# An mLSTM mixer's causal table added chunk by chunk, one maximum with a scalar operand, one scaling on ScalarE

## The chip, the core and the metric

One core of a Trainium2 chip runs the whole program. The metric is the device time of one execution, in microseconds (us). The core has five engines that run side by side, each in the order of its own queue: TensorE (PE, with its weight loads as PEld), VectorE (DVE), ScalarE (ACT), GpSimd (POOL) and SyncE (SP), which here issues the DMAs.

## What is computed

Two decoder layers, each a pre-normed mixer with two head groups in parallel: sliding-window attention and four mLSTM heads, both gated and joined by one output projection. The change lies in the mLSTM, which is computed in chunks of time:

```
D = where(causal, b[t] - b[s] + log_i[s], NEG)            # exponents of a chunk
m_t = maximum(a_t, D.max(-1))
S = (q k^T) * exp(D - m_t)
num = exp(a_t - m_t) * (q C_in) + S v
den = exp(a_t - m_t) * (q n_in) + S.sum(-1)
h = num / maximum(abs(den), exp(-m_t))
h = rms_norm(h, out_norm_g)                               # over the 256 values of a head
C, n, m = state after the chunk                           # scan over the chunks
```

There are 1040 rows of time (16 meta tokens and 1024 tokens), 4 heads with keys of 128 and values of 256.

## The kernel before

All matmuls that need fp32 accuracy are split: each operand is a high part and a low part, both rounded to a faster 32-bit format, and three matmuls take the place of one. ACT makes the high part by a copy, POOL or DVE the low part by a subtraction. Weights come in by DMA (`raw`), ACT copies the high part into `RING` (L159), and POOL subtracts (L160). A projection (L183) is a chain of 24 matmuls into one of two PSUM banks `pj`; an engine must read the bank out before the next but one projection can begin. These readers are L793 (values), L819 (inputs of the convolution) and L838, L841 and L842 (gates).

Time is cut into nine chunks: chunk 0 has the 16 meta rows, chunks 1 to 8 have 128 rows each. A layer runs the attention first, interleaved with its projections, and then, head by head, the mLSTM. `weave` puts the small tasks of one head's mLSTM (`m_tasks`) between the projections that the next head needs (`v_tasks`, `conv_tasks`) and those of the gates (`mo_tasks`). The tasks of a head are `begin`, and then `sa(c)`, `sb(c - 1)` and `sc_(c - 2)` for each chunk.

`begin` (L857) allocates `EB`, 128 partitions by 9 chunks by 128 columns. One DMA fills it with the negated running maxima of the head, the same on every partition, from a scratch tensor `em` in DRAM. Then one addition on POOL (L861) adds the causal table `tri` (0 where s <= t, -1e30 elsewhere) to all nine chunks at once.

`sa(c)` splits the values (ACT L877, POOL L878), turns and scales the keys (L881, L883, L884), updates the state (L887, then L891), splits the queries (L896, L897), takes the exponential of the chunk's part of `EB` (ACT L899), multiplies it with the scores (L901, L902) and splits the product (L905, L906).

`sb(c)` splits the state for the next chunk (ACT L911, POOL L912), multiplies the scores with the values and the queries with the state (both L867), and joins the two in `num` (ACT L925, DVE L929): 256 columns of values and in column 256 the sum `den`. A chain on one column follows, in a tile `s4` of four columns: the larger of `-den` and the bound (DVE L932), the larger of that and `den` (DVE L933), the reciprocal (L934), the sum of squares of the row (ACT L935), two steps of arithmetic (L936, L937), a power of -1/2 on POOL (L938), a product (L939), and last the scaling of the 256 columns of `num` by the result (DVE L941). `sc_(c)` turns the scaled rows on TensorE (L951), and ACT writes them out with the norm's weight (L954).

DVE also computes the convolution (L821, L824, L827), of which ACT's tanh (L826) is a part, and POOL multiplies with the gates (L606).

What sets the order: in the attention stage TensorE's instructions keep the order of the program (`pin`). In the mLSTM stage they do not: there a planner at compile time sets the order on every engine, by priority in the order of the program and by its own estimate of when each instruction can start. On the chip each engine then keeps to that order: an instruction that has to wait holds all that stands behind it in its queue.

Of the kernel before, what the change touches and what calls it, by code (L numbers as in the profile page):

```python
# [14 lines left out]
AF = mybir.ActivationFunctionType  # L15
ALU = mybir.AluOpType
# [46 lines left out]
def build(ctx, tc, I, O):  # L63
    nc = tc.nc
    ve, sc, gp, pe, sy = nc.vector, nc.scalar, nc.gpsimd, nc.tensor, nc.sync
    in_order = [False]

    def pin(ins):

        return tc.keep_in_program_order(ins) if in_order[0] else ins  # L70
# [25 lines left out]
    def bank(tag):  # L96
        return bp[tag].tile([128, 512], F32, name=tag)
# [22 lines left out]
    def unit(dt=F32):  # L120
        return up.tile([128, UW], dt, name="u")
# [4 lines left out]
    def p512(dt, n=512):  # L126
        return ptp.tile([128, 516], dt, name="p512")[:, :n]

    def w1k(dt=F32):
        return wkp.tile([128, 272], dt, name="w1k")  # L130
# [11 lines left out]
    tri = cp.tile([128, 128], F32, name="tri")  # L142
# [210 lines left out]
    for l in range(DEPTH):  # L353
# [500 lines left out]
        def m_tasks(h, st):  # L854
            live = {}

            def begin():  # L857
                EB = unit()[:, :].rearrange("p (c t) -> p c t", c=9)
                st["EB"] = EB
                sy.dma_start(EB, em[l].rearrange("(c h) t -> h c t", h=4)[h].partition_broadcast(128))  # L860
                gp.tensor_tensor(EB, EB, tri.rearrange("p (a t) -> p a t", a=1).to_broadcast([128, 9, 128]),  # L861
                                 op=ALU.add)
                st["Y"] = [unit() for _ in range(2)]

            def mm_split(out, a, b):
                for i, (x, y) in enumerate(((a[0], b[0]), (a[0], b[1]), (a[1], b[0]))):
                    pin(pe.matmul(out, x, y, start=(i == 0), stop=(i == 2)))  # L867

            def sa(c):
                t0, p = TT[c]  # L870
                r = 4 * c + h
                C0, C1 = Cb[c % 3], Cb[(c + 1) % 3]
                v = st["V"](c)[:p, :]
                qc, kc = st["q"][:, t0:t0 + p], st["k"][:, t0:t0 + p]
                KQ, VV = p512(F32R), p512(F32R, 516)
                V = VV[:p, 0:258], VV[:p, 258:516]
                sc.activation(V[0], v, AF.Copy)  # L877
                gp.tensor_tensor(V[1], v, V[0], op=ALU.subtract)  # L878
                if c < 8:
                    pk = bank("pt")  # L880
                    pin(pe.transpose(pk[:p, 0:128], kc, ident))  # L881
                    kt = KQ[:p, 0:128], KQ[:p, 128:256]
                    sc.activation(kt[0], pk[:p, 0:128], AF.Copy, scale=TK[:p, 2, r:r + 1])  # L883
                    ve.scalar_tensor_tensor(kt[1], pk[:p, 0:128], TK[:p, 2, r:r + 1], kt[0],  # L884
                                            ALU.mult, ALU.subtract)
                    pu = bank("pss")
                    mm_split(pu[:, 0:258], kt, V)  # L887
                    if c == 0:
                        ve.tensor_copy(C1, pu[:, 0:258])
                    else:  # L890
                        ve.scalar_tensor_tensor(C1, C0, AC[:, r:r + 1], pu[:, 0:258], ALU.mult, ALU.add)  # L891
                if c < first_q:
                    return
                q = KQ[:, 256:256 + p], KQ[:, 384:384 + p]
                if c > 0:
                    sc.activation(q[0], qc, AF.Copy)  # L896
                    gp.tensor_tensor(q[1], qc, q[0], op=ALU.subtract)  # L897
                De = w1k()
                sc.activation(De[:p, :p], st["EB"][:p, c, :p], AF.Exp, bias=TK[:p, 3, r:r + 1])  # L899
                pS = bank("pss")  # L900
                pin(pe.matmul(pS[:p, :p], kc, qc, start=True, stop=True))  # L901
                ve.tensor_tensor(De[:p, :p], pS[:p, :p], De[:p, :p], op=ALU.mult)  # L902
                DR = w1k(F32R)
                dr_ = DR[:p, 0:p], DR[:p, 128:128 + p]
                sc.activation(dr_[0], De[:p, :p], AF.Copy)  # L905
                ve.tensor_tensor(dr_[1], De[:p, :p], dr_[0], op=ALU.subtract)  # L906
                live[c] = q, V, dr_

            def split_state(c):
                ch, cl = Cr[c % 2]  # L910
                sc.activation(ch, Cb[c % 3], AF.Copy)  # L911
                gp.tensor_tensor(cl, Cb[c % 3], ch, op=ALU.subtract)  # L912

            def sb(c):
                if c + 1 < 9:
                    split_state(c + 1)
                if c < first_q:
                    return
                t0, p = TT[c]
                r = 4 * c + h  # L920
                q, V, dr_ = live.pop(c)
                num = w1k()
                pn = bank("po")
                mm_split(pn[:p, 0:258], dr_, V)
                sc.activation(num[:p, 0:257], pn[:p, 0:257], AF.Copy)  # L925
                if c > 0:
                    pi = bank("po")
                    mm_split(pi[:p, 0:258], q, Cr[c % 2])
                    ve.scalar_tensor_tensor(num[:p, 0:257], pi[:p, 0:257], TK[:p, 0, r:r + 1],  # L929
                                            num[:p, 0:257], ALU.mult, ALU.add)  # L930
                s4 = sm.tile([128, 4], F32, name="s4", bufs=4)
                ve.tensor_scalar(s4[:p, 0:1], num[:p, 256:257], -1.0, TK[:p, 1, r:r + 1], ALU.mult, ALU.max)  # L932
                ve.tensor_tensor(s4[:p, 0:1], s4[:p, 0:1], num[:p, 256:257], op=ALU.max)  # L933
                ve.reciprocal(s4[:p, 0:1], s4[:p, 0:1])  # L934
                sc.activation(pn[:p, 0:256], num[:p, 0:256], AF.Square, accum_out=s4[:p, 1:2])  # L935
                ve.tensor_scalar(s4[:p, 1:2], s4[:p, 1:2], s4[:p, 0:1], s4[:p, 0:1], ALU.mult, ALU.mult)  # L936
                ve.tensor_scalar(s4[:p, 1:2], s4[:p, 1:2], MV * EPS, None, ALU.add)  # L937
                gp.tensor_tensor(s4[:p, 2:3], s4[:p, 1:2], nhalf[:p, 0:1], op=ALU.pow)  # L938
                ve.tensor_scalar(s4[:p, 2:3], s4[:p, 2:3], s4[:p, 0:1], math.sqrt(MV) * 0.25,  # L939
                                 ALU.mult, ALU.mult)  # L940
                ve.tensor_scalar(num[:p, 0:256], num[:p, 0:256], s4[:p, 2:3], None, ALU.mult)  # L941
                live[c] = num

            def sc_(c):
                if c < first_q:
                    return
                t0, p = TT[c]
                hs = live.pop(c)
                ph = bank("pt")
                for f in range(2):  # L950
                    pin(pe.transpose(ph[:, 128 * f:128 * f + p], hs[:p, 128 * f:128 * f + 128], ident[:p, :p]))  # L951
                for f in range(2):
                    u = 2 * h + f
                    sc.activation(st["Y"][f][:, t0:t0 + p], ph[:, 128 * f:128 * f + p], AF.Copy,  # L954
                                  scale=cw[:, l, 40 + u:41 + u])

            out = [begin]
            for c in range(11):
                if c < 9:
                    out.append(lambda c=c: sa(c))  # L960
                if 0 <= c - 1 < 9:
                    out.append(lambda c=c - 1: sb(c))
                if 0 <= c - 2 < 9:
                    out.append(lambda c=c - 2: sc_(c))
            return out
# [105 lines left out]
        Cb = [CX[:, 288 * i:288 * i + 258] for i in range(3)]  # L1071
        Cr = [(CR[:, 516 * i:516 * i + 258], CR[:, 516 * i + 258:516 * i + 516]) for i in range(2)]
        weave(v_tasks(1, wv[1], M[1]) + conv_tasks(1, wc[1], M[1]), m_tasks(0, M[0]))
        for h in (1, 2):
            weave(mo_tasks(2 * h - 2, wo[2 * h - 2], M[h - 1]) + mo_tasks(2 * h - 1, wo[2 * h - 1], M[h - 1]) +
                  v_tasks(h + 1, wv[h + 1], M[h + 1]) + conv_tasks(h + 1, wc[h + 1], M[h + 1]),
                  m_tasks(h, M[h]))
        held = []
        mt = m_tasks(3, M[3])
        weave(mo_tasks(4, wo[4], M[2]) + mo_tasks(5, wo[5], M[2]) + mo_tasks(6, wo[6], M[3], held) +  # L1080
              mo_tasks(7, wo[7], M[3], held), mt[:-4])
# [8 lines left out]
        for i, k in enumerate(order):  # L1090
            ylo[k] = unit(F32R)
            for c, (t0, n, _) in enumerate(CH):
                a = s0 if c == 0 else t0
# [18 lines left out]
        for grp in (range(first_q, 5), range(5, 9)):  # L1112
            for hf in range(2):
# [25 lines left out]
                for t in grp:  # L1139
                    for i, k, w in tail:  # L1140
                        product(i, k, t, w)
                    t0, p = TT[t]
# [40 lines left out]
```

## Time and profile before

| | us |
|---|---|
| median of 3 runs | 2018.02 (2017.27 to 2020.26) |
| profiled execution | 2017.04 |
| its span, first to last instruction | 2015.3 |
| TensorE busy in the span | 1926.3 |
| mLSTM stage of layer 0, about | 440 to 850 |
| mLSTM stage of layer 1, about | 1430 to 1835 |
| L861, eight times | 2.62 to 3.00 each |

In the profile's rows a group is named by line, engine, operation, and tiles as out<-in, with partitions x elements. In tables of groups the busy time, the mean duration in ns and the idle time of the engine just before follow, with what ended it. In views in order of time the columns are start, duration, engine and line, and in brackets the idle time before with its releaser. The name of a tile can be that of its pool: `u` is a unit such as `EB`, `w1k` holds `num`, `s` is `s4`, `p` the split operands.

### The profile page before, as it was taken

The numbers are of one execution on the slowest core, as the hardware profiler recorded it, in microseconds if no ns is written. First come the engines' busy times: TensorE is split into PE (matmuls) and PEld (weight loads), VectorE is DVE, ScalarE is ACT, GpSimd is POOL, SyncE is SP. The second block draws the span as 40 slices with busy tenths as digits, with TensorE's granted clock in tenths as the row PEclk, the third lists the DMA queues.
The fourth block names the chain that finished last, engine by engine and source line by source line (L and its number), as shares of the span: only waits on it lengthen the run. The fifth ranks groups of instructions, "written<-read, shape, count | busy, mean of one in ns | idle before, by whom it ended". The sixth has DMA issues, their size and how long they took to land. (4 is left out here: it accounts for less than half of the span.)

```text
span 2015.3 us, 36021 instructions
## 1 busy us (share of the span) xinstructions
PE 1926.3 (96%) x12823; PEld 1815.1 (90%) x12823; DVE 1151.2 (57%) x3037; ACT 1032.5 (51%) x3065; POOL 913.0 (45%) x1052
## 2 busy tenths in 40 slices
PE   6999899999999999999999999999999999999899
PEld 6999899989999999867889999999999999998787
DVE  7767767667556464531535678775673736547111
ACT  5567767745353434542334678776454434346221
POOL 7544544335454445552325345443355443547331
PEclk9999999999999999999999999999999999999999
DMA  5111111121212121453442111111122221216443
GB/s 159 43 35 43 39 41 37 36 61 35 56 47 61 40 61 57 127 168 124 158 148 55 47 35 53 42 40 53 38 57 61 44 63 45 55 51 220 151 141 105
DMA packets 149795, 147.71 MB, mean 73 GB/s; under 512 B 14952, under 2 KB 122768, under 8 KB 149616
## 3 DMA queue, kind: packets, MB, share of 16 engines
q1 hardware_dynamic: 149616, 145.41, 24.7%
q8 instruction: 101, 1.65, 0.3%
q14 instruction: 78, 0.64, 0.1%
HBM read 122.01 MB, written 23.29 MB: 72 GB/s over the span
## 5 line engine op out<-in xcount | busy, mean ns | idle before, releaser
L183 PE MATMUL pj<-H,RING 128*128 128x384 f32 (+2 forms) x3456 | 584.0, 325 | 9.2 <-ACT u L819 9.2
L183 PEld LDWEIGHTS pj<-H,RING 128*128 128x128 f32 x3456 | 551.8, 191 | 12.7 <-ACT u L819 10.3
L160 POOL TENSOR_TENSOR RING<-raw,RING 128x512 fp32r<-128x512 f32 (+1 forms) x196 | 261.1, 1341 | 135.2 <-ACT RING L159 116.4
L222 PE MATMUL pj<-RING,H 128*128 128x256 f32 (+1 forms) x1920 | 269.8, 287 | 1.9 <-DVE w1k L190 1.9
L222 PEld LDWEIGHTS pj<-RING,H 128*128 128x128 f32 x1920 | 243.8, 190 | 2.4 <-DVE w1k L190 2.2
L222 PE MATMUL pj<-H,RING 128*128 128x384 f32 (+2 forms) x1152 | 218.6, 328 | 2.6 <-DVE u L564 2.5
L183 PE MATMUL pj<-RING,H 128*128 128x256 f32 x1536 | 203.1, 286 | 2.1 <-DVE H L292 1.4
L175 POOL TENSOR_TENSOR RING<-raw,RING 128x512 fp32r<-128x512 f32 x88 | 115.2, 1313 | 195.2 <-ACT RING L174 191.8
L183 PEld LDWEIGHTS pj<-RING,H 128*128 128x128 f32 x1536 | 190.6, 190 | 3.5 <-DVE H L292 1.6
L222 PEld LDWEIGHTS pj<-H,RING 128*128 128x128 f32 x1152 | 181.4, 192 | 3.5 <-PE T L668 1.3
L174 ACT ACTIVATE RING<-raw 128x512 fp32r<-128x512 f32 x128 | 80.7, 632 | 201.0 <-DMA raw<-in_w_out_dram 131.7
L159 ACT ACTIVATE RING<-raw 128x512 fp32r<-128x512 f32 (+1 forms) x196 | 122.6, 629 | 70.4 <-DMA raw<-in_w_in_dram 45.7
L713 POOL TENSOR_TENSOR u<-u,w1k 128x128 f32<-128x128 f32 (+1 forms) x136 | 64.0, 471 | 178.2 <-DVE w1k L709 167.0
L175 DVE TENSOR_TENSOR RING<-raw,RING 128x512 fp32r<-128x512 f32 x40 | 31.6, 791 | 195.0 <-ACT RING L174 195.0
L649 ACT ACTIVATE t<-S,mx 128x145 f32<-128x145 f32 (+1 forms) x272 | 100.6, 374 | 63.7 <-DVE mx L646 56.9
L679 POOL TENSOR_SCALAR_AFFINE_SELECT p<-p 128x512 fp32r<-128x512 f32 x112 | 72.4, 646 | 133.1 <-DVE p L675 130.0
L878 POOL TENSOR_TENSOR p<-u,p 128x258 fp32r<-128x258 f32 x64 | 46.3, 723 | 175.3 <-ACT p L877 172.7
L1131 PE MATMUL pj<-RING,H 128*128 128x512 f32 x352 | 113.4, 402 | 6.9 <-DVE p L1153 6.1
L824 DVE SCALAR_TENSOR_TENSOR t<-u,cw,t 128x384 f32<-128x384 f32 (+1 forms) x144 | 118.7, 824 | 2.2
L1131 PE MATMUL pss<-RING,H 128*128 128x512 f32 x352 | 113.6, 402 | 1.8 <-ACT H L1100 0.9
L628 PE MATMUL S<-u 128*128 128x272 f32 (+2 forms) x544 | 87.6, 280 | 19.3 <-DVE u L563 16.6
L654 ACT ACTIVATE t<-t,mx 128x144 f32<-128x144 f32 (+1 forms) x272 | 97.6, 406 | 14.9 <-DVE mx L651 14.6
(342 smaller groups left out, 3832.4 us busy)
## 6 DMA issues: line engine op xcount, KB each, us to landing
raw<-in_w_out_dram SPq DMA_DIRECT2D x128, 256.0 KB, 2.7
raw<-in_w_in_dram SPq DMA_DIRECT2D x100, 256.0 KB, 2.8
raw<-in_w_in_dram SPq DMA_DIRECT2D x192, 128.0 KB, 2.3
spool<-u SPq DMA_DIRECT2D x56, 192.0 KB, 1.9
p<-x SPq DMA_DIRECT2D x24, 256.0 KB, 4.2
t<-spool SPq DMA_DIRECT2D x28, 192.0 KB, 3.7
p<-spool SPq DMA_DIRECT2D x28, 192.0 KB, 3.8
u<-em SPq DMA_DIRECT2D x8, 576.0 KB, 6.6
```

Source lines behind the costliest of these rows:

```text
L159: sc.activation(hi, raw[:, :, 0:o], AF.Copy)
L160: eng.tensor_tensor(lo, raw[:, :, 0:o], hi, op=ALU.subtract)
L174: sc.activation(hi, raw, AF.Copy)
L175: (ve if i % 3 == 2 else gp).tensor_tensor(lo, raw, hi, op=ALU.subtract)
L183: pin(pe.matmul(out, a, b, start=(i == 0), stop=(i == n - 1)))
L222: pin(pe.matmul(out(), x, y, start=(k + i == 0), stop=(k == n - 1 and i == 2)))
L628: pin(pe.matmul(S[:p, h, o + 2 - 2 * h:o + 2 - 2 * h + kn], lq, Ks[i][:, k0:k0 + kn], start=(i == 0), stop=(i == 1)))
L649: sc.activation(P[:p, 145 * h:145 * h + 145], S[:p, h, 1 + 127 * h:146 + 127 * h], AF.Exp, bias=mx[:p, 0, h:h + 1], accum_out=mx[:p, 1, h: ...
L654: sc.activation(Pn, Pn, AF.Copy, scale=mx[:p, 2, h:h + 1])
L679: gp.affine_select(OW, HL, [[0, 4], [1, 128]], ALU.is_ge, 0.0, base=0, channel_multiplier=-1)
L824: ve.scalar_tensor_tensor(z, RAW[:, t0 + i:t0 + i + n], wcol(i), z, ALU.mult, ALU.add)
L1131: pin(pe.matmul(ps[:p, :], a, b, start=(i + n == 0), stop=(i == 15 and n == len(terms) - 1)))
```

## The change

Three edits, all in `m_tasks`. The addition of `tri` is made for each chunk by itself: `begin` adds it to chunk 0, and `sa(c)` adds it, as its first instruction, to chunk c + 1. A head now has nine additions of 128x128 in place of one of 128x1152. The maximum L933 takes `den` as a scalar operand per partition in place of a second tensor. And the scaling of `num` is an ACT copy with a scale per partition in place of a DVE multiplication.

```diff
                 sy.dma_start(EB, em[l].rearrange("(c h) t -> h c t", h=4)[h].partition_broadcast(128))
-                gp.tensor_tensor(EB, EB, tri.rearrange("p (a t) -> p a t", a=1).to_broadcast([128, 9, 128]),
-                                 op=ALU.add)
+                mask_eb(0)
                 st["Y"] = [unit() for _ in range(2)]
+
+            def mask_eb(c):
+                gp.tensor_tensor(st["EB"][:, c], st["EB"][:, c], tri, op=ALU.add)
...
                 C0, C1 = Cb[c % 3], Cb[(c + 1) % 3]
+                if c < 8:
+                    mask_eb(c + 1)
                 v = st["V"](c)[:p, :]
...
                 ve.tensor_scalar(s4[:p, 0:1], num[:p, 256:257], -1.0, TK[:p, 1, r:r + 1], ALU.mult, ALU.max)
-                ve.tensor_tensor(s4[:p, 0:1], s4[:p, 0:1], num[:p, 256:257], op=ALU.max)
+                ve.tensor_scalar(s4[:p, 0:1], s4[:p, 0:1], num[:p, 256:257], None, ALU.max)
...
-                ve.tensor_scalar(num[:p, 0:256], num[:p, 0:256], s4[:p, 2:3], None, ALU.mult)
+                sc.activation(num[:p, 0:256], num[:p, 0:256], AF.Copy, scale=s4[:p, 2:3])
                 live[c] = num
```

## The prediction, as it was made

> **What bounds the kernel now.** I read the page first, then TensorE's waits by stage, then the order of time around each wait. The page's first part, engine by engine (busy us, share of the span):
>
> ```profile
> PE 1926.3 (96%) x12823; PEld 1815.1 (90%) x12823; DVE 1151.2 (57%) x3037; ACT 1032.5 (51%) x3065; POOL 913.0 (45%) x1052
> ```
>
> TensorE is the bound, so an edit of DVE, ACT and POOL work pays only where TensorE now stands still. All edited lines run in the mLSTM stage, once per layer. Busy time in the two stretches (columns PE, PEld, DVE, ACT, POOL, clock, DMA share, GB/s):
>
> ```profile
> 440.00:850.00 410.00, 398.42 (x2714) 388.38 (x2713) 233.72 (x629) 190.19 (x580) 196.81 (x230) 0.99 0.22 59
> 1430.00:1835.00 405.00, 394.83 (x2704) 387.54 (x2703) 225.02 (x594) 186.92 (x554) 193.78 (x223) 0.99 0.23 61
> ```
>
> TensorE is idle for 11.6 and 10.2 us there: some 21.8 us, 1.1% of the run, is all that these edits can win. Who TensorE waited for in layer 0's stretch, then in layer 1's (us in total, times, longest):
>
> ```profile
> PE pt L951 <- DVE w1k L941: 4.4, 3, 3.0
> PE pj L183 <- ACT u L819: 3.3, 2, 1.7
> PE pss L867 <- POOL p L878: 1.5, 1, 1.5
> PE po L867 <- DVE w1k L929: 1.1, 1, 1.1
> ```
>
> ```profile
> PE pj L183 <- ACT u L819: 6.0, 3, 2.1
> PE pss L867 <- POOL p L878: 2.4, 1, 2.4
> PE po L867 <- DVE w1k L929: 1.1, 1, 1.1
> ```
>
> Ten lone stalls, beside the two of L929 at the ends of the stretches. The order of time tells what they share. Head 2 of layer 0 (start, duration, engine, line):
>
> ```profile
> 618.74 1.53 DVE L824 SCALAR_TENSOR_TENSOR t<-u,cw,t 128x384 f32<-128x384 f32 x1
> 619.82 2.98 POOL L861 TENSOR_TENSOR u<-u,tri 128x1152 f32<-128x1152 f32 x1
> 620.20 2.62 DVE L933 TENSOR_TENSOR s<-s,w1k 128x1 f32<-128x1 f32 x1
> 622.74 1.71 DVE L824 SCALAR_TENSOR_TENSOR t<-u,cw,t 128x384 f32<-128x384 f32 x1
> 622.76 1.28 POOL L160 TENSOR_TENSOR RING<-raw,RING 128x512 fp32r<-128x512 f32 x1
> 624.48 0.52 ACT L826 ACTIVATE t<-t 128x384 f32<-128x384 f32 x1 [5.24 <-DVE t L824]
> 624.91 0.47 ACT L819 ACTIVATE u<-pj 128x384 f32<-128x384 f32 x1
> 625.44 3.29 PE L183 MATMUL pj<-H,RING 128*128 128x272 f32 x24 [1.70 <-ACT u L819]
> ```
>
> L933 handles one element per partition and takes 2.62 us: it ends as POOL's L861 ends, at 622.80. [...] So L824 is late, so the tanh L826 behind it, so ACT's queue, in which the eviction L819 stands behind L826, so TensorE, which needs that bank. Head 1 of each layer, layer 0 first:
>
> ```profile
> 506.18 4.63 DVE L941 TENSOR_SCALAR w1k<-w1k,s 128x256 f32<-128x256 f32 x1
> 506.81 2.62 POOL L861 TENSOR_TENSOR u<-u,tri 128x1152 f32<-128x1152 f32 x1
> 509.40 1.25 POOL L160 TENSOR_TENSOR RING<-raw,RING 128x512 fp32r<-128x512 f32 x1
> 510.86 0.44 PE L951 MATMUL pt<-cst,w1k 128*128 128x128 f32 x2 [2.97 <-DVE w1k L941]
> ```
>
> ```profile
> 1494.59 2.98 POOL L861 TENSOR_TENSOR u<-u,tri 128x1152 f32<-128x1152 f32 x1
> 1495.15 2.84 DVE L824 SCALAR_TENSOR_TENSOR t<-u,cw,t 128x384 f32<-128x384 f32 x1
> 1499.77 0.50 PE L183 MATMUL pj<-H,RING 128*128 128x256 f32 x2 [2.05 <-ACT u L819]
> ```
>
> L941, of one SBUF operand, stood from 506.18 until POOL's L861 and the L160 behind it were both done. Head 0 stalls differently: L861 holds POOL's own queue.
>
> ```profile
> 454.92 2.66 POOL L861 TENSOR_TENSOR u<-u,tri 128x1152 f32<-128x1152 f32 x1 [10.00 <-DMA u<-em]
> 457.54 0.73 POOL L878 TENSOR_TENSOR p<-u,p 128x258 fp32r<-128x258 f32 x1
> 458.32 0.50 PE L867 MATMUL pss<-p,p 128*128 128x258 f32 x2 [1.47 <-POOL p L878]
> ```
>
> The other stalls of L819 and L951 show the same order, each within 10 us of the start of its head's L861. So the whole sum of the waits on L941, L819 and L878, 4.4 + 3.3 + 1.5 + 6.0 + 2.4 = 17.6 us, hangs on the eight L861: 13.7 us by the port in heads 1 to 3, 3.9 us by POOL's queue in head 0.
>
> **The change, part by part.** The groups that it touches, on DVE, ACT and POOL (busy us, mean ns | idle before, releaser):
>
> ```profile
> L941 DVE TENSOR_SCALAR w1k<-w1k,s 128x256 f32<-128x256 f32 (+1 forms) x68 | 39.2, 576 | 1.4
> L933 DVE TENSOR_TENSOR s<-s,w1k 128x1 f32<-128x1 f32 (+1 forms) x68 | 34.8, 512 | 1.5
> L939 DVE TENSOR_SCALAR s<-s 128x1 f32<-128x1 f32 (+1 forms) x68 | 14.3, 210 | 36.7 <-POOL s L938 36.7
> ```
>
> ```profile
> L935 ACT ACTIVATE po<-w1k 128x256 f32<-128x256 f32 (+1 forms) x68 | 26.2, 385 | 17.3 <-DVE w1k L929 15.3 <-DVE u L785 0.9
> L899 ACT ACTIVATE w1k<-u,TK 128x128 f32<-128x128 f32 (+1 forms) x68 | 26.4, 388 | 13.9 <-POOL u L861 13.9
> L905 ACT ACTIVATE w1k<-w1k 128x128 fp32r<-128x128 f32 (+1 forms) x68 | 20.3, 299 | 21.3 <-DVE w1k L902 20.6
> L826 ACT ACTIVATE t<-t 128x384 f32<-128x384 f32 (+1 forms) x48 | 23.7, 493 | 95.2 <-DVE t L824 94.9
> ```
>
> ```profile
> L861 POOL TENSOR_TENSOR u<-u,tri 128x1152 f32<-128x1152 f32 x8 | 22.8, 2855 | 20.1 <-DMA u<-em 20.1
> L713 POOL TENSOR_TENSOR u<-u,w1k 128x128 f32<-128x128 f32 (+1 forms) x136 | 64.0, 471 | 178.2 <-DVE w1k L709 167.0
> ```
>
> *The table, 8 additions made 72.* A piece is 128x128 fp32; L713 is POOL's row of that shape, 471 ns. So a head costs 9 x 0.471 = 4.24 us instead of 2.855, and POOL gets 72 x 0.471 - 22.8 = +11.1 us. POOL is busy for half of these stretches, so the 11.1 us hide in its idle time, unless the pieces stand in front of something urgent (second rival). The gain: no DVE instruction waits for more than one piece, some 0.47 us, where it now waits for up to 2.98. That gives back up to 2.5 us at each of heads 1 to 3. The stalls there are 1.6 to 2.1 us, and 3.0 at the L941 of head 1. What is late next is L824 behind L160's 1.28 us; no wait for L819 in these stretches comes from that alone, since all five lie behind an L861. I leave 1.5 us of the 13.7 for pieces that fall close together: 12.2 us gained, between 6 (half of them) and 13.7. In head 0 the wait for the DMA stays; L878 then stands behind one to three pieces (0.47 to 1.41 us) instead of 2.66, which gains 1.25 to 2.19 of each stall and no more than the stall itself: I take 1.4 of the 1.5 and 1.6 of the 2.4, 3.0 us. ACT's L899 waits for its own piece only, which is asked for one chunk ahead.
>
> [...]
>
> *The maximum, L933.* With a scalar operand it takes what L939, which has one too, takes: 210 ns, whatever POOL does meanwhile (minimum, median and maximum in ns):
>
> ```profile
> L939 DVE TENSOR_SCALAR s<-s x68: 195/214/217, 463.2 to 1833.8; 128x1 f32<-128x1 f32 x64, 16x1 f32<-16x1 f32 x4
> ```
>
> DVE saves 34.8 - 14.3 = 20.5 us, of which only the waits behind L861 were on the path, and these are in the 13.7. Nothing is added.
>
> *The scaling, L941 from DVE to ACT.* DVE loses 39.2 us. ACT's price: L935 does the same 128x256 without a scalar from SBUF in 385 ns; such a scalar costs L899 - L905 = 388 - 299 = 89 ns. So 474 ns, x68 = 32.2 us, on an engine that is under 47% busy here. It adds a wait to ACT's queue: L941 waits for L939, which waits for POOL's L938 (36.7 us in all), and behind it stand the evictions L819, L793, L838 and L841 that TensorE needs. Upper bound of what ACT loses: 32.2 + 36.7 = 68.9 us. Which part of it reaches TensorE? ACT now waits for DVE for 94.9 + 20.6 + 15.3 = 130.8 us (L824, L902, L929), and TensorE for L819 for 3.3 + 6.0 = 9.3 of them: 7%. By that share 4.8 us; but none of the 9.3 lies away from an L861, which would make it 0. I take half, 2.4 us, with 0 and 15 (the gain's own size) as the ends.
>
> [...]
>
> **The sum.** The profiled execution took 2017.04 us, of which 2015.3 are its span. 2017.04 - 12.2 - 3.0 + 2.4 = 2004.2. The median shown, 2018.02, stands 0.98 above the profiled execution; on that footing the forecast is **2005 us**.
>
> **The rivals.**
>
> *Pieces in a row.* The DMA lands, all nine pieces are ready at once, and POOL does them one behind the other, 4.24 us. For: L160 took over from L861 at 509.40 with L941 still waiting. Against: L933 and L824 got in between L861 and L160 at 622.8. Then L938 and L878 come 1.4 us later than now. The L819 stalls stay (9.3), L941's go (4.4), head 0's grow by 2 x 1.4 = 2.8, ACT costs its 2.4: 2018.0 - 4.4 + 2.8 + 2.4 = 2019, no change.
>
> *ACT becomes the place of the stall* (slower). L941 waits in ACT's queue with an eviction behind it. For: L826 does that now, with waits of 5.2 us. Against: 53% of ACT is free, and the 7%. It decides from 15.2 / 68.9 = 22% of ACT's loss on the path; at a third it is 23 us: 2018.0 - 15.2 + 23 = 2026.
>
> *The L861 is not the cause.* The planner lays out the same lateness again, with other work (L160, 1.3 us) in the port's way; or it reorders TensorE's work with it: half of the 15.2 is won, less 2.4: 2018.0 - 7.6 + 2.4 = 2013.
>
> **How the numbers follow.** The forecast gets 0.68, the three rivals 0.11, 0.11 and 0.10. A measurement of this kernel can tell 0.2%, 4 us. Faster by more than that: the forecast, and six tenths of the third rival, 0.74. The same: the second half of the first and third, 0.13. Slower: the ACT case and what the first one has beyond 2022, 0.13. The range starts where all 17.6 us and some of the tails' waits go and ACT costs nothing, 1999, and reaches to the no-change case, 2019; left out are the ACT case and the far end of the first rival.
>
> **What would show it.** In the profile after: TensorE's waits on L941's successor and on L819 under 3 us in both stretches; POOL's pieces at 0.45 to 0.5 us each, spread over several us per head; L933 at 0.21 us with no 2.6 us among them; L824's mean of 0.82 us lower; ACT's scaling at about 0.47 us. I am wrong if a TensorE wait on L819, L838 or L793 of 1 to 2 us stands where ACT waits for L939, or if the waits are gone and the time is not.

## The result, and the profile after

The changed kernel takes 1995.26 us (median of 4 runs, 1994.39 to 2000.37) against 2017.64 for the kernel before (median of 4): a ratio of 0.989, 95% interval 0.987 to 0.991. That is 22 us less. The forecast was 13 less, 2005, in a range from 1999 to 2019, and the measured time lies below that range: the direction was right, the size was not. The profiled execution took 1995.97 us, its span 1994.2. The page's first part:

```profile
PE 1916.2 (96%) x12823; PEld 1806.1 (91%) x12823; DVE 1099.9 (55%) x2969; ACT 1062.6 (53%) x3133; POOL 929.9 (47%) x1116
```

TensorE runs the same 12823 matmuls and is busy for 10 us less (1926.3 before). Fewer waits cannot do that, since a wait is not counted as busy. The matmuls themselves ran faster, and this was the part that the prediction had left out. First the waits, layer 0's stage (438 to 831 us) and then layer 1's (1416 to 1802), with what TensorE waited for, us in total, times, longest:

```profile
PE pss L1135 <- ACT H L1104: 1.3, 1, 1.3
PE pss L869 <- POOL p L882: 1.2, 1, 1.2
PE po L869 <- DVE w1k L933: 1.1, 1, 1.1
PE pss L869 <- DVE w1k L906: 0.7, 1, 0.7
PE pj L183 <- DVE w1k L190: 0.5, 1, 0.5
PE pj L183 <- ACT t L838: 0.3, 1, 0.3
```

```profile
PE pss L869 <- POOL p L882: 2.0, 1, 2.0
PE pj L1135 <- ACT H L1104: 1.3, 1, 1.3
PE po L869 <- DVE w1k L933: 1.1, 1, 1.1
PE pj L183 <- ACT u L793: 0.3, 1, 0.3
```

(Lines behind the edits have moved by up to four: L867 is now L869, L878 L882, L929 L933, L933 L937, L941 L945.) Every wait for L819 and for the scaling is gone. What is left of the 17.6 us that hung on the eight long additions is the wait for L882 in head 0, 3.2 us.

Then the clock. Three stretches of 3.41 us each in the kernel before, around the stall in head 1 of layer 0 (columns: stretch, length, busy PE, PEld, DVE, ACT, POOL, granted clock, DMA share, GB/s):

```profile
507.97:511.38 3.41, 0.52 (x4) 0.49 (x5) 3.41 (x3) 0.15 (x1) 2.68 (x2) 1.00 0.13 34
511.38:514.80 3.42, 3.42 (x17) 3.42 (x17) 3.19 (x12) 2.74 (x9) 1.48 (x2) 0.50 0.31 77
514.80:518.21 3.41, 3.41 (x29) 3.41 (x28) 3.38 (x11) 1.84 (x5) 0.62 (x1) 1.00 0.29 79
```

TensorE stands still for 2.9 us in the first stretch. In the second it is busy throughout, but at a granted clock of 0.50, and it runs 17 matmuls where the third holds 29. So the stall cost its idle time and half of the next 3.41 us, 1.7 us more. Head 1 of layer 1 is the same:

```profile
1497.84:1501.25 3.41, 1.48 (x12) 1.48 (x13) 2.88 (x7) 2.90 (x9) 3.04 (x3) 1.00 0.28 71
1501.25:1504.66 3.41, 3.41 (x17) 3.23 (x17) 3.20 (x10) 1.24 (x4) 1.05 (x2) 0.50 0.35 90
```

while 1.6 us of idle time had no such end (head 3 of layer 0):

```profile
733.25:736.66 3.41, 1.83 (x14) 1.61 (x14) 3.23 (x8) 1.55 (x5) 2.27 (x3) 1.00 0.22 56
736.66:740.07 3.41, 2.71 (x23) 2.49 (x21) 3.24 (x5) 1.11 (x4) 1.29 (x1) 1.00 0.20 53
```

The half-clock periods begin on a grid of 3.41 us that runs through the whole execution: those that begin at 511.38 and at 1501.25 in the profile before, 989.87 us apart, are 290 steps of 3.413 us from each other. In this profile five lie in the two mLSTM stages, each behind a stall that one of the eight long additions had caused; in the profile after there is none. (Each of the two profiles has one more just behind the end of a stage, after the wait at the start of the output projection.) The other three of the eight stalls had no such end: 1.70 and 1.58 us in heads 2 and 3 of layer 0, and 2.40 us in head 0 of layer 1, which lay across two windows of the grid, 0.7 us in one and 1.7 in the next. So it also depends on where a stall falls on the grid, and that five of the eight paid is the count of this one execution.

TensorE need not stand still for all of a window: in the one from 1497.84 to 1501.25 it was idle for 1.9 of 3.41 us, and a granted clock of 0.50 followed.

The groups that the change touches, after it (busy us, mean ns | idle before):

```profile
L865 POOL TENSOR_TENSOR u<-u,tri 128x128 f32<-128x128 f32 x72 | 42.1, 618 | 21.3 <-DMA u<-em 21.3
L937 DVE TENSOR_SCALAR s<-s,w1k 128x1 f32<-128x1 f32 (+1 forms) x68 | 14.3, 210 | 1.7
L945 ACT ACTIVATE w1k<-w1k,s 128x256 f32<-128x256 f32 (+1 forms) x68 | 34.5, 508 | 38.4 <-DVE s L943 37.5 <-ACT p L887 0.3
L824 DVE SCALAR_TENSOR_TENSOR t<-u,cw,t 128x384 f32<-128x384 f32 (+1 forms) x144 | 109.1, 757 | 2.6
```

### The profile page after: what moved, and what is told of

It reads as the page before. It is cut to its first block, busy times and chain, and to the rows that moved or that the text cites. A ratio compares the mean times of both kernels' runs of the same rounds, so it can differ in the third digit from the quotient of the medians.

```text
span 1994.2 us, 36168 instructions
## 1 busy us (share of the span) xinstructions
PE 1916.2 (96%) x12823; PEld 1806.1 (91%) x12823; DVE 1099.9 (55%) x2969; ACT 1062.6 (53%) x3133; POOL 929.9 (47%) x1116
## 5 line engine op out<-in xcount | busy, mean ns | idle before, releaser
L160 POOL TENSOR_TENSOR RING<-raw,RING 128x512 fp32r<-128x512 f32 (+1 forms) x196 | 260.6, 1337 | 137.8 <-ACT RING L159 125.4
L159 ACT ACTIVATE RING<-raw 128x512 fp32r<-128x512 f32 (+1 forms) x196 | 122.9, 629 | 73.3 <-DMA raw<-in_w_in_dram 48.2
L882 POOL TENSOR_TENSOR p<-u,p 128x258 fp32r<-128x258 f32 x64 | 46.7, 730 | 169.2 <-ACT p L881 169.1
L824 DVE SCALAR_TENSOR_TENSOR t<-u,cw,t 128x384 f32<-128x384 f32 (+1 forms) x144 | 109.1, 757 | 2.6
L628 PE MATMUL S<-u 128*128 128x272 f32 (+2 forms) x544 | 87.5, 280 | 19.3 <-DVE u L563 16.3
```

The lines of the kernel that those rows point to most:

```text
L159: sc.activation(hi, raw[:, :, 0:o], AF.Copy)
L160: eng.tensor_tensor(lo, raw[:, :, 0:o], hi, op=ALU.subtract)
L628: pin(pe.matmul(S[:p, h, o + 2 - 2 * h:o + 2 - 2 * h + kn], lq, Ks[i][:, k0:k0 + kn], start=(i == 0), stop=(i == 1)))
L824: ve.scalar_tensor_tensor(z, RAW[:, t0 + i:t0 + i + n], wcol(i), z, ALU.mult, ALU.add)
```

## The experiments

Two questions were open: whether the half-clock periods carry the missing 9 us, and which of the three edits does the work. All ratios are against the kernel before on the same chip. "Stage" is the sum of both mLSTM stages in the profiled execution, from the second pair of transposes in `gates` (L745) to the first matmul of the output projection; "idle" is TensorE's idle time in it, "half" its time at half clock, and "rest" is stage - idle - half / 2. The prediction and the expectations speak of a port that POOL holds and DVE needs. No run shows a port. The traces show only the outcome: a DVE instruction that stands until a POOL instruction has ended, in the profile before for 2.62 to 4.63 us, one in each of heads 1 to 3 of both layers. Not every one stands: there L906, with two operands from SBUF, ran in 0.29 us (503.86) while POOL's tensor_tensor L938 took 0.72 (503.62).

| kernel | ratio, 95% interval | stage | idle | half | rest |
|---|---|---|---|---|---|
| before | 1 | 798.9 | 21.7 | 17.1 | 768.6 |
| changed | 0.9892 (0.9874 to 0.9910) | 777.3 | 9.7 | 0.0 | 767.6 |
| split_only | 0.9937 (0.9925 to 0.9949) | 787.8 | 14.9 | 6.8 | 769.5 |
| max_only | 0.9982 (0.9971 to 0.9993) | 797.2 | 22.4 | 10.2 | 769.7 |
| scale_only | 1.0007 (0.9998 to 1.0016) | 798.6 | 25.9 | 3.5 | 770.9 |
| max_scale | 1.0001 (0.9989 to 1.0014) | 795.7 | 22.6 | 6.8 | 769.7 |
| split_max | 0.9962 (0.9949 to 0.9975) | 789.1 | 16.7 | 10.2 | 767.2 |
| split_scale | 0.9919 (0.9904 to 0.9934) | 779.1 | 11.1 | 0.5 | 767.7 |
| three_pieces | 0.9963 (0.9951 to 0.9976) | 788.8 | 17.9 | 3.4 | 769.2 |
| mask_twice | 1.0094 (1.0079 to 1.0109) | 815.8 | 35.2 | 23.9 | 768.7 |
| vm_on_dve | 0.9898 (0.9885 to 0.9912) | 776.8 | 9.6 | 0.0 | 767.2 |
| vm_128 | 0.9917 (0.9903 to 0.9931) | 778.4 | 9.8 | 0.1 | 768.5 |
| mask_on_dve | 0.9982 (0.9974 to 0.9991) | 794.9 | 20.2 | 10.2 | 769.6 |
| after_vm_128 | 0.9908 (0.9892 to 0.9924) | 776.7 | 7.8 | 3.4 | 767.1 |

The last column answers the first question. The stage runs from 776.7 to 815.8 us, a spread of 39, and the rest stays between 767.1 and 770.9. So in all fourteen profiles the stage is a constant amount of matmul work plus idle time plus half of the half-clock time. One profile stands for each kernel, and the executions of a kernel differ: those of the kernel before that the ratios rest on go from 2010 to 2022 us, with a mean granted clock from 0.991 down to 0.984. Outside the stages, which the edits hardly touch, the fourteen profiles took 1213.9 to 1221.8 us, of which 34 to 53 at half clock. A difference of a few us between two ratios need not come from the stages.

### The edits one by one

split_only: the table chunk by chunk, and nothing else.

```diff
-                gp.tensor_tensor(EB, EB, tri.rearrange("p (a t) -> p a t", a=1).to_broadcast([128, 9, 128]),
-                                 op=ALU.add)
+                mask_eb(0)
...
+                if c < 8:
+                    mask_eb(c + 1)
```

> Only the table is added chunk by chunk; the maximum and the scaling stay as before. Port theory (the eight long POOL additions hold the port that DVE needs, and each long TensorE stall is followed by 3.4 us at half clock): most of the 22 us come from this edit alone, 1996 to 2001 us, no half-clock period behind the heads' starts, TensorE's waits on L819 under 2 us in all. Load theory (the gain is DVE's 60 us less work): under 4 us of gain, 2014 or more.

Measured: 12.7 us of gain (0.0063 of 2014.59): more than half of the change, less than the port theory wanted. One stall of 4.1 us was left in head 1 of layer 0.

max_only: the maximum alone.

```diff
-                ve.tensor_tensor(s4[:p, 0:1], s4[:p, 0:1], num[:p, 256:257], op=ALU.max)
+                ve.tensor_scalar(s4[:p, 0:1], s4[:p, 0:1], num[:p, 256:257], None, ALU.max)
```

> Only the maximum takes a scalar operand. Port theory: L824 takes over the wait that L933 had behind the long addition, so the stalls stay, 2013 to 2018 us. Load theory: DVE has 20 us less work, a third of the gain, 2010 us.

Measured: 0.998, as the port theory expected (the load theory's 2010 us would be 0.996, outside the interval). Head 2 of layer 0 shows that the standstill only moves on by one instruction, from the maximum to L824:

```profile
617.06 2.98 POOL L861 TENSOR_TENSOR u<-u,tri 128x1152 f32<-128x1152 f32 x1
617.44 0.20 DVE L933 TENSOR_SCALAR s<-s,w1k 128x1 f32<-128x1 f32 x1
617.56 2.90 DVE L824 SCALAR_TENSOR_TENSOR t<-u,cw,t 128x384 f32<-128x384 f32 x1
620.49 0.53 ACT L826 ACTIVATE t<-t 128x384 f32<-128x384 f32 x1 [3.78 <-DVE t L824]
```

scale_only and max_scale: the scaling on ACT alone, and together with the maximum.

```diff
-                ve.tensor_scalar(num[:p, 0:256], num[:p, 0:256], s4[:p, 2:3], None, ALU.mult)
+                sc.activation(num[:p, 0:256], num[:p, 0:256], AF.Copy, scale=s4[:p, 2:3])
```

> Only the scaling moves to ScalarE. Port theory: the one stall of 2.97 us on L941 goes, with its half-clock period, 4 to 5 us of gain, 2012 to 2015 us; the stalls on L819 stay. Load theory: DVE has 39 us less work, two thirds of the gain, 2003 us. If ScalarE's queue suffers: above 2018.

> The maximum and the scaling as in the changed kernel, the table still added at once. Port theory: 2010 to 2015 us, the stalls on L819 stay with their half-clock periods. Load theory: nearly all of the gain, 1995 to 2000 us.

Measured: no gain in either. The port theory's 4 to 5 us for scale_only did not come: other instructions stood behind the long addition instead (stalls of 3.0 and 3.5 us on L929), and the table shows more idle time than before. The load theory falls with max_scale: DVE has 60 us less work, and nothing is faster.

### The edits by twos

split_max leaves the scaling on DVE, split_scale leaves the maximum a tensor_tensor.

> The changed kernel with the scaling left on DVE. Port theory: within 2 us of the changed kernel, 1995 to 1998 us, since a piece of 0.47 us holds L941 up by no more than that. If ScalarE's new work costs TensorE what the prediction allowed (2.4 us), this is 2 us faster than the changed kernel, 1993.

> The changed kernel with the maximum left as a tensor_tensor. Port theory: within 2 us of the changed kernel, 1995 to 1998 us. If the maximum carries a part of its own: 2000 us or more.

split_scale does not decide: its median, 2000.9 us, is what the second theory named, but its interval (0.992) overlaps the changed kernel's and its stage is 1.8 us longer. Its profile has a stall of 3.1 us on L838 in head 1 of layer 1 that the changed kernel does not have, and in front of that ACT waited 4.1 us for a DMA of weights (L159), not for the maximum. Whether the maximum carries a part of its own stays open.

split_max contradicts the port theory: 0.996, 14 us short of the changed kernel's gain. Its profile shows, in head 1 of layer 1, what the port theory could not explain, one DVE instruction standing through eleven POOL instructions:

```profile
1491.82 1.05 POOL L882 TENSOR_TENSOR p<-Vm,p 16x258 fp32r<-16x258 f32 x1
1492.20 5.75 DVE L945 TENSOR_SCALAR w1k<-w1k,s 128x256 f32<-128x256 f32 x1
1492.84 3.73 POOL L865 TENSOR_TENSOR u<-u,tri 128x128 f32<-128x128 f32 x9
1496.54 1.25 POOL L160 TENSOR_TENSOR RING<-raw,RING 128x512 fp32r<-128x512 f32 x1
1498.00 0.69 PE L955 MATMUL pt<-cst,w1k 128*128 128x128 f32 x2 [5.11 <-DVE w1k L945]
```

The nine pieces run in a row there, 0.44 us each with starts 0.41 apart, and none lets DVE in. In the changed kernel nine pieces run in a row as well, in head 1 of both layers, but they take 4.92 us (layer 0) and 5.83 us (layer 1) instead of 3.73, and a dozen DVE instructions run among them, in layer 0 these for instance:

```profile
502.64 0.64 DVE L824 SCALAR_TENSOR_TENSOR t<-u,cw,t 128x384 f32<-128x384 f32 x1
503.21 0.55 DVE L910 TENSOR_TENSOR w1k<-w1k 128x128 fp32r<-128x128 f32 x1
503.68 0.47 DVE L933 SCALAR_TENSOR_TENSOR w1k<-po,TK,w1k 128x257 f32<-128x257 f32 x1
```

```profile
501.67 4.92 POOL L865 TENSOR_TENSOR u<-u,tri 128x128 f32<-128x128 f32 x9
506.56 1.60 POOL L160 TENSOR_TENSOR RING<-raw,RING 128x512 fp32r<-128x512 f32 x1
```

The kind of DVE instruction did not decide it: in split_only it was a tensor_tensor (L910) that stood for 5.35 us, in layer 0 of split_max an L824 that stood for 5.61. What these had in common was the POOL instruction at their start, L882 on `Vm`: the low part of the 16 rows of chunk 0, the one such split of each head that uses 16 partitions instead of 128. The kernel before has it too: its L941, which stood for 4.63 us through two more POOL instructions, had begun behind the same subtraction (L878 there). In all profiles taken up to then, the standstills of over 4 us began so. Two kernels, both made from split_max, put this to the test.

vm_on_dve moves that subtraction to DVE; vm_128 leaves it on POOL but makes it 128 partitions wide, with rows of zeros.

```diff
-                gp.tensor_tensor(V[1], v, V[0], op=ALU.subtract)
+                (gp if c else ve).tensor_tensor(V[1], v, V[0], op=ALU.subtract)
```

```diff
-            Vm = sm.tile([16, 258], F32, name="Vm")
+            Vm = sm.tile([128, 258], F32, name="Vm")
+            ve.memset(Vm, 0.0)
...
+                pv = p if c else 128
-                v = st["V"](c)[:p, :]
+                v = st["V"](c)[:pv, :]
...
-                sc.activation(V[0], v, AF.Copy)
-                gp.tensor_tensor(V[1], v, V[0], op=ALU.subtract)
+                W = VV[:pv, 0:258], VV[:pv, 258:516]
+                sc.activation(W[0], v, AF.Copy)
+                gp.tensor_tensor(W[1], v, W[0], op=ALU.subtract)
```

> The kernel with split table and scalar maximum (scaling on DVE), in which the low part of the 16-row values of chunk 0 is subtracted on DVE instead of POOL. In the profile of that kernel DVE stands still for 5.6 us through ten POOL instructions in a row, and every such row begins with this 16-partition subtraction. Theory that the 16-partition instruction sets off the standstill: the two stalls of 3.9 and 5.1 us go with their half-clock periods, about 12 us of gain on it, 1996 to 2000 us. Rival, that a DVE instruction of one SBUF operand never gets in between POOL's pieces: the stalls stay, 2006 to 2010 us.

> The same kernel with that subtraction left on POOL, but over 128 partitions (the values of chunk 0 padded with rows of zeros, which no matmul reads). POOL's time for it should stay about 0.73 us. Theory of the 16 partitions: no standstill over several POOL instructions any more, 1996 to 2000 us. Rival, that any POOL work in front of the pieces does it: 2006 to 2010 us.

Measured: 0.990 and 0.992 against 0.996 for split_max, and both intervals overlap the changed kernel's. vm_128 is the sharper of the two: the same instruction on the same engine at the same cost (0.79 us), with pieces in a row right behind it, and now DVE gets in between them.

```profile
503.67 0.79 POOL L885 TENSOR_TENSOR p<-Vm,p 128x258 fp32r<-128x258 f32 x1
504.42 4.88 POOL L866 TENSOR_TENSOR u<-u,tri 128x128 f32<-128x128 f32 x8
```

```profile
503.78 1.09 DVE L825 SCALAR_TENSOR_TENSOR t<-u,cw,t 128x384 f32<-128x384 f32 x1
504.80 0.54 DVE L948 TENSOR_SCALAR w1k<-w1k,s 128x256 f32<-128x256 f32 x1
505.27 0.47 DVE L936 SCALAR_TENSOR_TENSOR w1k<-po,TK,w1k 128x257 f32<-128x257 f32 x1
```

Over all the profiles with that subtraction on 16 partitions, a DVE instruction stood at its end with more POOL work right behind it ten times, and ten times it stood on, through one to ten POOL instructions; with 128 partitions this came up twice, both in vm_128, and both times DVE went ahead at once (L825, 1.09 us, and L948, 0.83). The width is not all there is to it, though. In head 0 of layer 1 of vm_128 a DVE instruction that takes 0.28 us elsewhere stood through three changes between POOL instructions that all use 128 partitions:

```profile
1440.62 0.67 POOL L885 TENSOR_TENSOR p<-u,p 128x258 fp32r<-128x258 f32 x1
1440.84 2.41 DVE L913 TENSOR_TENSOR w1k<-w1k 128x128 fp32r<-128x128 f32 x1
1441.22 0.49 POOL L904 TENSOR_TENSOR p<-u,p 128x128 fp32r<-128x128 f32 x1
1441.64 1.46 POOL L919 TENSOR_TENSOR u<-u 128x258 fp32r<-128x258 f32 x2
```

So the split of the table does not need the scaling on ACT for its gain. With split_max's order DVE happened to stand behind the 16-partition subtraction with the nine pieces right after it. In the changed kernel's order the nine pieces of head 1 run before that subtraction (501.67 against 511.28 in layer 0, 1482.20 against 1487.99 in layer 1). Why 16 partitions do it, no run here shows.

### Size and place of the addition

three_pieces adds the table to three chunks at a time; mask_twice is the kernel before with the long addition made twice; mask_on_dve has the nine pieces on DVE.

```diff
-                gp.tensor_tensor(st["EB"][:, c], st["EB"][:, c], tri, op=ALU.add)
+                gp.tensor_tensor(st["EB"][:, c:c + 3], st["EB"][:, c:c + 3],
+                                 tri.rearrange("p (a t) -> p a t", a=1).to_broadcast([128, 3, 128]), op=ALU.add)
...
-                if c < 8:
-                    mask_eb(c + 1)
+                if c in (1, 4):
+                    mask_eb(c + 2)
```

> The changed kernel with three additions of 384 columns per head instead of nine of 128. A piece should take about 1.0 us. If a stall and its half-clock period come only where the hold exceeds the slack of the chain: as fast as the changed kernel, 1994 to 1998 us. If a hold costs in proportion to its length: a third of the gain is lost, 2002 us.

Measured: 0.996, a gain of 7 us, so two thirds of the change's gain are lost; neither theory's number holds. A piece takes 1.25 us, and stalls of 1.2 to 2.0 us on L838 stand in heads 1 to 3. In head 2 of layer 0 the chain of the convolution waits three times: L821 behind a piece of 1.33 us (1.17 us instead of 0.5), and two L824 behind an L160 of 1.41 us each (1.53 us instead of 0.6); L826, L838 and TensorE follow.

```diff
+                gp.tensor_tensor(EB, EB, tri.rearrange("p (a t) -> p a t", a=1).to_broadcast([128, 9, 128]),
+                                 op=ALU.add)
```

> The kernel before with the long addition made twice in a row (the table's zeros and -1e30 doubled, which leaves the exponentials as they are). Idle time alone: each of the eight stalls grows by 2.6 to 3.0 us, 8 x 2.9 = 23 us, 2041 us. With the clock: also the three stalls that had no half-clock period behind them get one, 1.7 us each, and some periods double, 2044 to 2052 us.

Measured: 1.009, 19 us more, less than either number. The stages grow by 16.9 us: idle time by 13.5 and half of the half-clock time by 3.4, from 17.1 to 23.9 us. So the second addition, 2.7 us long, costs TensorE 1.7 us of idle time on average, and not the 2.9 that was expected. The division into idle time and clock holds; the sizes were guessed too high.

```diff
-                gp.tensor_tensor(st["EB"][:, c], st["EB"][:, c], tri, op=ALU.add)
+                ve.tensor_tensor(st["EB"][:, c], st["EB"][:, c], tri, op=ALU.add)
```

> The changed kernel with the nine pieces per head on DVE instead of POOL. A piece has two SBUF operands of 128 columns, as L906 has, so 0.29 us, 72 x 0.29 = 21 us more DVE work; POOL loses 42 us. If POOL's hold of the port is all there is: as fast as the changed kernel or up to 3 us faster, 1991 to 1997 us. If DVE's load matters: above 2000 us. In head 0 DVE instead of POOL now waits for the DMA of the maxima, 10 us.

Measured: 0.998, the gain is nearly gone, as the expectation had it for the case that DVE's load matters. DVE does not have to wait for POOL's additions now, but does them itself, 22.6 us in all, 367 ns each, ahead of the convolution: TensorE waits for L838 for 8.5 us, and for L888 in head 0, where DVE and no longer POOL waits for the DMA, for 5.1.

after_vm_128 is the changed kernel with vm_128's edit.

> The changed kernel with the subtraction of the 16-row values over 128 partitions. Its profile has no standstill over several POOL instructions, so nothing is left to win there: within 2 us of the changed kernel, 1993 to 1998 us. Faster by 3 us or more would mean that executions differ in this.

Measured: 0.991, its interval overlaps the changed kernel's, as expected. No version here is shown to be faster than the changed kernel.

## Why the prediction was wrong in size and right in kind

*Which stalls go.* Right. All the stalls that the prediction hung on the eight long additions are gone but for 3.2 us in head 0, and split_only and max_scale show that the addition, not DVE's load, was their cause. The port, to which the prediction puts down 13.7 of the 17.6 us, is in no run: what the profile before shows in its place is a DVE instruction (L933, L824 or L941) that ended with the long addition or up to 1.4 us behind its end.

*The price of a stall.* This is the step that failed. The prediction took TensorE's idle time, some 21.8 us, for all that these edits can win, and put each stall in the sum at its idle time alone: 12.2 + 3.0 us gained, less 2.4 for ACT, 12.8. It put nothing for the half clock behind a stall, 17.1 us in the stages. The idle time in the stages fell by 21.7 - 9.7 = 12.0 us. But the stage fell by 21.6: half of 17.1 us at half clock, 8.5, went with the stalls, and 1.0 is left over in the rest. Outside the stages 0.5 us came back, which makes the span's 21.1. That the idle time itself came so close to the sum, 12.0 against 12.8, is in part luck, since the terms were off both ways: the stalls of heads 1 to 3 gave all of their 13.7 instead of 12.2, head 0 gave 0.7 instead of 3.0, ACT took some 0.3 instead of 2.4, and other waits grew by about 2 (0.7 for L906 and 0.9 at the starts of the output projection among them). The clue stood in a row that the prediction quotes: a clock of 0.99 over 815 us, 1% of which is 8 us. A stage's clock below 1.00 behind lone stalls belongs to the price of these stalls.

*The split's cost.* Mis-sized. A piece took 618 ns on average and not 471: about 0.45 us where pieces followed each other undisturbed, up to 0.78 where a DVE instruction came in between. POOL got 42.1 - 22.8 = 19.3 us and not 11.1. In heads 1 to 3 that stayed hidden. In head 0 the prediction had L878 behind one to three pieces, 0.47 to 1.41 us. Seven and eight stood in front of it (layer 0, then layer 1), longer than the one addition of 2.66 us before, and so this term gave 3.9 - 3.2 = 0.7 us instead of 3.0:

```profile
455.07 2.93 POOL L865 TENSOR_TENSOR u<-u,tri 128x128 f32<-128x128 f32 x7 [11.04 <-DMA u<-em]
457.96 0.73 POOL L882 TENSOR_TENSOR p<-u,p 128x258 fp32r<-128x258 f32 x1
```

```profile
1433.27 3.35 POOL L865 TENSOR_TENSOR u<-u,tri 128x128 f32<-128x128 f32 x8 [10.23 <-DMA u<-em]
```

*"No DVE instruction waits for more than one piece."* True in the changed kernel, and not in general: split_only and split_max show 5.4 to 5.8 us. The third of the change that looked like a side matter, the scaling on ACT, made the difference between 0.996 and 0.989 only through the order that came with it.

*The maximum.* Right in its price, 210 ns, and by itself worth little, 0.998. Together with the split its part is not settled (split_scale).

*The scaling on ACT.* It costs 508 ns, not 474, and ACT waits for L943 for 37.5 us, close to the 36.7 of the bound. What reached TensorE was 0.3 us on L838, not 2.4. The prediction's other end, 0, was the better choice: vm_on_dve, which leaves the scaling on DVE and has no standstill of 5 us, has practically the same stage, 776.8 us against 777.3.

*The rivals.* Pieces in a row: they did come in a row, nine in 4.92 us, but in heads 1 to 3 of the changed kernel DVE gets in between. Behind the 16-partition subtraction it does not, and split_max, at 0.996, comes nearest to this rival; in head 0 POOL's subtraction did start later (457.96 against 457.54 in layer 0), but the stall did not grow. ACT as the place of the stall did not come about. That the addition is not the cause is refuted by split_only, 12.7 us, and by mask_twice, 19 us the other way.

## What to carry to other kernels

On a TensorE-bound kernel, price a lone stall at more than its idle time (here 1.7 us more behind five of eight stalls): look at the granted clock just behind it, in stretches of a few microseconds and not in the stage's mean. Where POOL and DVE share work on SBUF, try POOL's long two-operand instructions in shorter pieces (split_only alone gained 12.7 us), and look at what stands in front of a row of them: in split_max, behind a subtraction on 16 partitions, a DVE instruction stood through the whole row, 5.75 us. An edit that helps only together with another one can be a sign that the order of the instructions, and not the edit, made the difference; a test that takes away what the order ran into tells the two apart.

## What the runs showed of the hardware that was not expected

- In these profiles TensorE's granted clock changed on a grid of 3.41 us, and a window in which TensorE was idle for about half the time was followed by one at a granted clock of 0.50, 1.7 us lost. Over the fourteen profiles (from 25 us on, counting windows at full clock) this happened after none of 134 windows with 1.0 to 1.4 us of idle time, 18 of 91 with 1.4 to 1.8, and 133 of 136 with more; in those before and after the change alone after none of 20, 3 of 10 and 20 of 20.
- Behind a POOL subtraction on 16 partitions (0.78 us on average in split_max) the following POOL instructions ran without a gap for a DVE instruction that already stood, which took up to 5.75 us; behind the same one on 128 partitions (0.79 us in vm_128) DVE went ahead, in 1.09 and 0.83 us. One DVE instruction in vm_128 stood for 2.41 us through 128-partition instructions alone.
- A DVE maximum of one element per partition took 138 to 2630 ns with two SBUF operands (68 in the profile before), 512 on average, and 200 to 216 with the second one as a scalar operand (68 in the profile after), whatever POOL did.
